# First RMS norm of a two-layer decoder: second tile of x transferred ahead of the weights, its statistics on another engine

## The chip, the cores and the metric

The kernel runs on one core of one Trainium2 chip. The metric is device time in microseconds (us) from the start to the end of one execution; lower is better. The core has TensorE (PE, matmuls and transposes), VectorE (DVE), ScalarE (ACT), GpSimd (POOL) and SyncE (SP, which issues most transfers); they run side by side, each through its own queue in order, and wait for each other through semaphores.

## The reference

Two decoder layers over x of 256 tokens by 1024 features, all in float32. Cut to what matters here:

```python
def rms_norm(x, g):
    y = x * lax.rsqrt(jnp.mean(x * x, axis=-1, keepdims=True) + NORM_EPS)
    return y * g

for l in range(DEPTH):                                  # 2
    h = rms_norm(x, attn_norm[l])                       # the norm of this change, for l = 0
    parts = jnp.split(h @ w_in[l], splits, axis=-1)     # 13 column groups
    # convolution module, compressed / selected / windowed attention, dilated attention
    x = x + jnp.concatenate([y_a, y_b, y_c], axis=-1) @ w_out[l]
    x = x + conv_ffn(rms_norm(x, ffn_norm[l]), w_up[l], ...)
```

## The kernel before

**Tiling.** x is held as two tiles of 128 tokens by 1024 features, called tile 0 and tile 1 (`x_sb[0]`, `x_sb[1]`). Each dense product is done as three matmuls on rounded halves: every operand is split into a high part (`hi`, written by ACT) and a remainder (`lo`, written by DVE as operand minus high part), and `dense3` (L441 to L443) adds hi*hi, hi*lo and lo*hi.

**Weights.** All weights lie in one stream of pieces, taken in order. A piece is transferred into one of four `raw` buffers (`raw_in`, L255), then `convert_piece` writes `whi` (ACT, L209) and `wlo` (DVE, L212) from it; the raw buffer is free for a later piece when `wlo` is written. Of layer 0, pieces 0 to 3 are the 280 columns of chunk `a0` (two of eight contraction blocks each, 280 KB), pieces 4 and 5 are `w1` (tile `w`, L282, 512 KB each, no split, buffers of their own), and pieces 6 to 9 are the 512 columns of chunk `a` (512 KB each). Piece 6 can so be issued when piece 0 has been split. `emit_piece` emits the next piece; `take` emits up to three pieces ahead.

**The first norm.** `norm_squares` sums the squares of a tile in two halves of 512 columns (tile 0: one half on ACT, one on DVE; tile 1: both on ACT). `norm_tile` then makes the mean, adds EPS, takes the inverse square root by a magic constant and three Newton steps (`rsqrt_into`; ten instructions on one column, named `na`, `nr`, `nwh`, `nwt`), scales each half by that and by the gain into `xn` (L222, DVE), transposes it in four 128x128 blocks on PE (L350, tile `tpx`) and splits the transposed half into `xT_hi` (ACT) and `xT_lo` (DVE). The gain of this norm lies in a PSUM bank: a matmul of a row of ones with the gain row (`gain`, L247) spreads it over the partitions. Matmuls of chunk `a0` for tile 0, then for tile 1, then those of chunk `a` follow (tile `A`).

**Order.** A planner orders the instructions of each engine when the kernel is built: it takes what it thinks ready, earlier lines first. `tc.issue_after(ins)` puts those instructions of its block that are on the engine of `ins` behind `ins` in that queue; it is order alone, not a wait. Pieces 0 and 1 are emitted between the squares of tile 1 and its `norm_tile`, piece 0 behind the scaling of tile 0 on DVE, piece 1 behind both splits of tile 0. SP's queue is in the order x tile 0, gain row, piece 0, x tile 1, pieces 1 to 3, then `w1`, the next gain, `w1`, piece 6, and after it the tables `feat`, `cst` and `ffeat` (339, 610 and 88 KB). POOL does little here: constants, small transfers, and `gain_tables` (tile `gsc`, twelve instructions for each layer, from the transferred `grow`, for which there is one buffer).

Of the kernel before, what the change touches and what calls it, by code (L numbers as in the profile page):

```python
# [12 lines left out]
F32 = mybir.dt.float32  # L13
F32R = mybir.dt.float32r
I32 = mybir.dt.int32
AF = mybir.ActivationFunctionType
ALU = mybir.AluOpType
AX = mybir.AxisListType

P = 128  # L20
D = 1024
# [6 lines left out]
EPS = 1e-6  # L28
BIG = 1e30
TAPS = 31  # L30
MAGIC = float(0x5F3759DF)
# [156 lines left out]
def tile_hybrid_trunk(ctx, tc, x_in, pos_in, stream, feats, gains, norms, const_in, out):  # L188
    nc = tc.nc
# [3 lines left out]
    sp = ctx.enter_context(tc.tile_pool(name="sp", bufs=2))  # L193
# [5 lines left out]
    def tp_bank(nm):  # L199
        return ps.tile([P, 512], F32, tag="tp", name=nm, bufs=2)  # L200
# [7 lines left out]
    def copy_act(o, i, **kw):  # L208
        return nc.scalar.activation(out=o, in_=i, func=AF.Copy, **kw)  # L209

    def tt(o, a, b, op):
        return nc.vector.tensor_tensor(out=o, in0=a, in1=b, op=op)  # L212

    def ts(o, a, s1, s2, op0, op1=None, eng=None):
        e = eng or nc.vector
        if op1 is None:
            e.tensor_scalar(out=o, in0=a, scalar1=s1, scalar2=None, op0=op0)
        else:
            e.tensor_scalar(out=o, in0=a, scalar1=s1, scalar2=s2, op0=op0, op1=op1)

    def stt(o, a, s, b, op0, op1):
        return nc.vector.scalar_tensor_tensor(out=o, in0=a, scalar=s, in1=b, op0=op0, op1=op1)  # L222
# [3 lines left out]
    def load_x(t):  # L226
        for h in range(2):
            nc.sync.dma_start(x_sb[t][:, h * 512:(h + 1) * 512], x_in[0, t * P:(t + 1) * P, h * 512:(h + 1) * 512])
# [21 lines left out]
    state = {"next": 0, "spare": {}, "gate": {}, "raw": {}}  # L250

    def raw_in(i):
        n = PIECES[i][3]
        raw = wp.tile([P, PIECE], F32, tag="raw", name=f"raw{i}", bufs=RAW_BUFS)
        nc.sync.dma_start(raw[:, :n], stream[OFFSETS[i]:OFFSETS[i] + P * n].rearrange("(p n) -> p n", p=P))  # L255
        return raw

    state["raw"][0] = raw_in(0)
    load_x(1)
    for i in (1, 2, 3):  # L260
        state["raw"][i] = raw_in(i)

    def slots(i):
# [37 lines left out]
        cursor["i"] += 1  # L301
        return emitted.pop(i)

    def rsqrt_into(y, a, shape, nm):
        h = sp.tile(shape, F32, tag="nwh", name=f"nwh{nm}", bufs=2)
        t = sp.tile(shape, F32, tag="nwt", name=f"nwt{nm}", bufs=2)
        ts(y.bitcast(I32), a.bitcast(I32), -0.5, MAGIC, ALU.mult, ALU.add)
        ts(h, a, -0.5, None, ALU.mult)
        one = shape[1] == 1
        for _ in range(3):  # L310
            if one:
                ts(t, y, y, h, ALU.mult, ALU.mult)
                ts(y, t, 1.5, y, ALU.add, ALU.mult)
            else:
                tt(t, y, y, ALU.mult)
                tt(t, t, h, ALU.mult)
                stt(y, t, 1.5, y, ALU.add, ALU.mult)
# [4 lines left out]
    def norm_squares(t, nm, out, split=False):  # L322
        x = x_sb[t]
        ss = sp.tile([P, 2], F32, tag="ss", name=f"ss{nm}", bufs=2)
        for h in range(2):
            sl = slice(h * 512, h * 512 + 512)
            if split and h:
                nc.vector.tensor_tensor_reduce(out=out[:, sl], in0=x[:, sl], in1=x[:, sl], op0=ALU.mult, op1=ALU.add, scale=1.0, scalar=0.0,
                                               accum_out=ss[:, h:h + 1])
            else:  # L330
                nc.scalar.activation(out=out[:, sl], in_=x[:, sl], func=AF.Square, accum_out=ss[:, h:h + 1])
        return ss

    def norm_tile(t, gi, nm, ss=None):
        x = x_sb[t]
        g = gain_tiles[gi]
        xn = sp.tile([P, D], F32, tag="xn", name=f"xn{nm}", bufs=1)
        if ss is None:
            ss = norm_squares(t, nm, xn)
        a = sp.tile([P, 1], F32, tag="na", name=f"na{nm}", bufs=2)  # L340
        ts(a, ss[:, 0:1], ss[:, 1:2], 1.0 / D, ALU.add, ALU.mult)
        ts(a, a, EPS, None, ALU.add)
        r = sp.tile([P, 1], F32, tag="nr", name=f"nr{nm}", bufs=2)
        rsqrt_into(r, a, [P, 1], nm)
        for h in range(2):
            sl = slice(h * 512, h * 512 + 512)
            scaled = stt(xn[:, sl], x[:, sl], r, g[:, sl], ALU.mult, ALU.mult)
            tp = tp_bank(f"tpx{nm}{h}")
            for k in range(4):
                nc.tensor.transpose(tp[:, k * P:(k + 1) * P], xn[:, h * 512 + k * P:h * 512 + (k + 1) * P], ident)  # L350
            tv = tp.rearrange("p (k c) -> p k c", k=4)
            hi = xT_hi[:, h * 4:h * 4 + 4, t * P:(t + 1) * P]
            lo = xT_lo[:, h * 4:h * 4 + 4, t * P:(t + 1) * P]
            ends = copy_act(hi, tv), tt(lo, tv, hi.bitcast(F32), ALU.subtract)
        return ends + (scaled,)
# [10 lines left out]
    nc.gpsimd.dma_start(freq, const_in[:, CONST_N:CONST_N + 32])  # L366
    junk = wp.tile([P, PIECE], F32, tag="whi", name="junk", bufs=W_BUFS)
    ss0 = norm_squares(0, "a00", junk, split=True)
    x_ready = norm_tile(0, 0, "a00", ss0)
    junk = wp.tile([P, PIECE], F32, tag="whi", name="junk1", bufs=W_BUFS)  # L370
    ss1 = norm_squares(1, "a01", junk)
    with tc.issue_after(x_ready[2].ins):
# [4 lines left out]
    for l in range(L):  # L377
        g = sp.tile([P, 4, 64], F32, tag="grow", name=f"grow{l}", bufs=1)
        nc.gpsimd.dma_start(g.rearrange("p a b -> p (a b)"), gains[l:l + 1, :].broadcast_to([P, 256]))
        grow.append(g)  # L380
    x_ready = norm_tile(1, 0, "a01", ss1)
    cos_t = cp.tile([P, 3, 32], F32, name="cos_t")
    sin_t = cp.tile([P, 3, 32], F32, name="sin_t")
    gs_t = []
# [108 lines left out]
    for l in range(L):  # L493
        f = sp.tile([P, NPF], F32, tag="feat", name=f"feat{l}", bufs=1)
# [318 lines left out]
        def conv_tail():  # L813
# [11 lines left out]
            ts(va, vp[:, 0:2], EPS, None, ALU.add)  # L825
            rs = mp.tile([P, 2], F32, name="rs")
            rsqrt_into(rs, va, [P, 2], f"ln{l}")
            dg = mp.tile([P, 2, P], F32, tag="cth", name="dg", bufs=1)
            bp = o_bank("lnb")
# [19 lines left out]
        def dil_qk(nm, jp):  # L849
            q = 2 if nm == "q" else 3  # L850
            dst = mp.tile([P, 3, S], F32, tag=f"d{nm}", name=f"d{nm}{jp}", bufs=1)
            dil_state[nm] = dst
            banks = tok_chunk(f"d{nm}{jp}", 384, False, f"D{nm}{jp}{l}")
            zrs = rope([b[:, 0:384] for b in banks], 6, q, (0, 1), f"d{nm}{jp}")
            for t in range(NT):
                tp = tp_bank(f"tpd{nm}{jp}{t}")
                for i in range(3):
                    nc.tensor.transpose(tp[:, i * P:(i + 1) * P], zrs[t][:, i * P:(i + 1) * P], ident)
                copy_act(dst[:, :, t * P:(t + 1) * P], tp[:, 0:384].rearrange("p (k c) -> p k c", k=3))
# [80 lines left out]
        for step in ORDER.split():  # L940
            nm, arg = step[:-1].split("(")
            arg = int(arg) if arg.isdigit() else arg.split(",")
            if nm == "dq":
                dil_qk("q", arg)
            elif nm == "dk":
                dil_qk("k", arg)
            else:
                dict(np=nsa_pair, t=conv_taps, nf=nsa_finish, dv=dil_v, da=dil_attn, ds=dil_scores, pv=dil_pv, ct=lambda _: conv_tail())[nm](arg)

# [25 lines left out]
        for t in range(NT):  # L975
            src = obs[t]
            for nh in range(2):
                sl = slice(nh * 512, nh * 512 + 512)
                tt(x_sb[t][:, sl], x_sb[t][:, sl], src[nh], ALU.add)
            ends = norm_tile(t, 2 * l + 1, f"f{l}{t}")  # L980
# [97 lines left out]
```

## Time and profile before

| | |
|---|---|
| median of 3 runs | 757.74 us (756.37 to 759.26) |
| profiled execution, time | 756.99 us |
| profiled execution, span from first to last instruction | 755.2 us |
| outside the span | 1.79 us |

The profile is of one execution. PE, DVE, ACT and POOL times are those of instructions; PEld is PE's weight load, beside its matmuls. A view by windows gives each engine's busy time in a stretch, with the count of instructions in brackets. The chain of waits follows the last instruction back, at each step to what released it. The ends of matmuls are modelled.

### The profile page before, as it was taken

How to read it: one execution, taken by the hardware profiler on the slowest of the kernel's cores; microseconds unless marked ns; L12 is line 12 of the kernel's file. 1: busy time of each engine (PE TensorE's matmuls, PEld its weight loads, DVE VectorE, ACT ScalarE, POOL GpSimd, SP SyncE). 2: the span in 40 equal slices, each digit the busy share in tenths (PEclk: the TensorE clock that was granted, in tenths of full speed). 3: DMA queues.
4: the chain of work that ended last, by engine and by line, in shares of the span. 5: the costliest groups of instructions: out<-in, count | busy, mean ns of one | idle time of the engine just before them, and what ended most of it. 6: DMA issues, size and time to landing. Idle time of an engine off the chain costs nothing.

```text
span 755.2 us, 13417 instructions
## 1 busy us (share of the span) xinstructions
PE 733.7 (97%) x4802; PEld 638.8 (85%) x4802; DVE 598.6 (79%) x1387; ACT 487.5 (65%) x1176; POOL 23.4 (3%) x57
## 2 busy tenths in 40 slices
PE   5999999999999999999999999999999999999997
PEld 4778776887899999988868977778789999999885
DVE  6889999986898888854487798998868988888441
ACT  3866998656586666643358589987538666666330
POOL 3300000000000000000040000000000000000000
PEclk9999999999999999999999999999999999999999
DMA  7754233245366656566447241235245665666631
GB/s 261 262 188 126 66 103 115 103 168 158 114 225 196 192 173 194 193 200 196 142 161 259 85 125 44 89 108 194 84 141 168 202 189 176 195 189 194 196 112 56
DMA packets 36005, 119.77 MB, mean 159 GB/s; under 512 B 4113, under 2 KB 4385, under 8 KB 35938
## 3 DMA queue, kind: packets, MB, share of 16 engines
q1 hardware_dynamic: 35714, 118.63, 49.2%
q8 instruction: 38, 0.62, 0.3%
q0 software_dynamic: 224, 0.28, 0.2%
q14 instruction: 29, 0.24, 0.1%
HBM read 117.85 MB, written 1.05 MB: 157 GB/s over the span
## 4 chain that ended last, share of the span: by engine, by line
PE 81%; DVE 8%; ACT 6%; DMA 3%; issue 2%; SPq 0%; DVEq 0%; ACTq 0%
PE up L442 10%; PE up L443 10%; PE up L441 10%; PE da L441 3%; PE da L442 3%; PE da L443 3%; PE db L441 3%; PE db L442 2%; PE db L443 2%; DVE wlo L212 2%; DMA raw<-in_stream 2%; ACT whi L209 2%; PE sc L742 1%; PE Dk L441 1%; PE Dk L443 1%
## 5 line engine op out<-in xcount | busy, mean ns | idle before, releaser
L212 DVE TENSOR_TENSOR wlo<-raw,whi 128x1024 fp32r<-128x1024 f32 (+3 forms) x232 | 259.8, 1125 | 88.8 <-ACT whi L209 88.1
L209 ACT ACTIVATE whi<-raw 128x1024 fp32r<-128x1024 f32 (+3 forms) x232 | 225.1, 980 | 108.7 <-PE db L443 54.5
L442 PE MATMUL up<-xT_lo,whi 128*128 128x256 f32 x640 | 178.9, 279 | 0.0
L443 PE MATMUL up<-xT_hi,wlo 128*128 128x256 f32 x640 | 178.9, 279 | 0.0
L441 PE MATMUL up<-xT_hi,whi 128*128 128x256 f32 x640 | 178.7, 279 | 0.0
L442 PEld LDWEIGHTS up<-xT_lo,whi 128*128 128x128 f32 x640 | 120.2, 188 | 0.0
L441 PEld LDWEIGHTS up<-xT_hi,whi 128*128 128x128 f32 x640 | 120.0, 188 | 0.0
L443 PEld LDWEIGHTS up<-xT_hi,wlo 128*128 128x128 f32 x640 | 119.9, 187 | 0.0
L222 DVE SCALAR_TENSOR_TENSOR u<-up,ffeat,u 128x255 f32<-128x255 f32 (+1 forms) x176 | 80.1, 479 | 2.6
L222 DVE SCALAR_TENSOR_TENSOR acc<-a_pad,dwh,acc 128x256 f32<-128x256 f32 x120 | 54.2, 480 | 0.3 <-ACT acc L706 0.2
L1031 ACT ACTIVATE sl<-u 128x256 f32<-128x256 f32 x44 | 18.1, 417 | 47.7 <-DVE u L222 47.7
L1024 ACT ACTIVATE u<-up,ffeat 128x256 f32<-128x256 f32 x88 | 44.2, 552 | 0.0
L441 PE MATMUL db<-whi,gT_hi 128*128 128x512 f32 x88 | 34.6, 393 | 0.0
L441 PE MATMUL da<-whi,gT_hi 128*128 128x512 f32 x88 | 34.6, 393 | 0.0
L442 PE MATMUL da<-wlo,gT_hi 128*128 128x512 f32 x88 | 34.4, 391 | 0.0
L442 PE MATMUL db<-wlo,gT_hi 128*128 128x512 f32 x88 | 34.4, 391 | 0.0
L443 PE MATMUL db<-whi,gT_lo 128*128 128x512 f32 x88 | 34.3, 390 | 0.0
L443 PE MATMUL da<-whi,gT_lo 128*128 128x512 f32 x88 | 34.3, 390 | 0.0
L441 PE MATMUL A<-whi,xT_hi 128*128 128x280 f32 (+1 forms) x64 | 23.2, 363 | 1.7 <-ACT xT_hi L209 1.7
L209 ACT ACTIVATE ms<-ms,dd 128x128 f32<-128x128 f32 (+1 forms) x64 | 24.3, 451 | 0.0
L443 PE MATMUL A<-whi,xT_lo 128*128 128x280 f32 (+1 forms) x64 | 22.9, 358 | 0.3 <-DVE xT_lo L212 0.3
L442 PE MATMUL A<-wlo,xT_hi 128*128 128x280 f32 (+1 forms) x64 | 23.0, 360 | 0.0
(342 smaller groups left out, 1572.7 us busy)
## 6 DMA issues: line engine op xcount, KB each, us to landing
raw<-in_stream SPq DMA_DIRECT2D x172, 512.0 KB, 4.1
raw<-in_stream SPq DMA_DIRECT2D x48, 384.0 KB, 3.1
raw<-in_stream SPq DMA_DIRECT2D x8, 280.0 KB, 4.3
w<-in_stream SPq DMA_DIRECT2D x4, 512.0 KB, 5.7
gain<-in_norms SPq DMA_DIRECT2D x3, 512.0 KB, 3.8
x<-in_x SPq DMA_DIRECT2D x4, 256.0 KB, 4.2
out<-x SPq DMA_DIRECT2D x4, 256.0 KB, 2.0
feat<-in_feats SPq DMA_DIRECT2D x2, 339.0 KB, 4.4
```

Source lines behind the costliest of these rows:

```text
L209: return nc.scalar.activation(out=o, in_=i, func=AF.Copy, **kw)
L212: return nc.vector.tensor_tensor(out=o, in0=a, in1=b, op=op)
L222: return nc.vector.scalar_tensor_tensor(out=o, in0=a, scalar=s, in1=b, op0=op0, op1=op1)
L441: nc.tensor.matmul(o, a_hi, b_hi, start=start, stop=False)
L442: nc.tensor.matmul(o, a_hi, b_lo, start=False, stop=False)
L443: nc.tensor.matmul(o, a_lo, b_hi, start=False, stop=stop)
L742: nc.tensor.matmul(sc[:, j * 512:j * 512 + n], QT[hp_, pair, P:2 * P], keys[hp_], start=True, stop=True)
L1024: nc.scalar.activation(out=u[:, h], in_=z, func=AF.Identity, scale=c[:, 2:3], bias=c[:, 3:4])
L1031: nc.scalar.activation(out=sl_, in_=u[:, 0], func=AF.Silu)
```

## The change

Tile 1 of x is transferred ahead of piece 0. The ten instructions on one column are taken out of `norm_tile` into `norm_rms`, which takes an engine; for tile 1 of the first norm that engine is POOL. The whole of that `norm_tile` is in a block that is queued behind `x_ready[1]`, the last `xT_lo` of tile 0: its DVE instructions, which are the two scalings and two `xT_lo`, come after it on DVE. Two single-operation instructions (adding EPS, and the product with -0.5) get a second operation, a product with 1.0, in every norm.

```diff
-    state["raw"][0] = raw_in(0)
     load_x(1)
-    for i in (1, 2, 3):
+    for i in range(4):
         state["raw"][i] = raw_in(i)
...
-    def rsqrt_into(y, a, shape, nm):
+    def rsqrt_into(y, a, shape, nm, eng=None):
...
-        ts(y.bitcast(I32), a.bitcast(I32), -0.5, MAGIC, ALU.mult, ALU.add)
-        ts(h, a, -0.5, None, ALU.mult)
+        ts(y.bitcast(I32), a.bitcast(I32), -0.5, MAGIC, ALU.mult, ALU.add, eng=eng)
+        ts(h, a, -0.5, 1.0, ALU.mult, ALU.mult, eng=eng)
...
-                ts(t, y, y, h, ALU.mult, ALU.mult)
-                ts(y, t, 1.5, y, ALU.add, ALU.mult)
+                ts(t, y, y, h, ALU.mult, ALU.mult, eng=eng)
+                ts(y, t, 1.5, y, ALU.add, ALU.mult, eng=eng)
...
+    def norm_rms(ss, nm, eng=None):
+        a = sp.tile([P, 1], F32, tag="na", name=f"na{nm}", bufs=2)
+        ts(a, ss[:, 0:1], ss[:, 1:2], 1.0 / D, ALU.add, ALU.mult, eng=eng)
+        ts(a, a, EPS, 1.0, ALU.add, ALU.mult, eng=eng)
+        r = sp.tile([P, 1], F32, tag="nr", name=f"nr{nm}", bufs=2)
+        rsqrt_into(r, a, [P, 1], nm, eng)
+        return r
...
-    x_ready = norm_tile(0, 0, "a00", ss0)
+    x_ready = norm_tile(0, 0, "a00", norm_rms(ss0, "a00"))
...
-    x_ready = norm_tile(1, 0, "a01", ss1)
+    with tc.issue_after(x_ready[1].ins):
+        x_ready = norm_tile(1, 0, "a01", norm_rms(ss1, "a01", nc.gpsimd))
```

## Rows read from the trace of the kernel before

**Rows 1.** The page: the span, and each engine's busy time in it.

```profile
span 755.2 us, 13417 instructions
PE 733.7 (97%) x4802; PEld 638.8 (85%) x4802; DVE 598.6 (79%) x1387; ACT 487.5 (65%) x1176; POOL 23.4 (3%) x57
```

**Rows 2.** Windows: busy PE, PEld, DVE, ACT, POOL; granted clock, DMA share, GB/s.

```profile
0.00:20.00 20.00, 12.01 (x44) 8.11 (x44) 12.31 (x40) 8.21 (x20) 7.11 (x25) 1.00 0.80 269
...
40.00:60.00 20.00, 20.00 (x112) 16.83 (x113) 17.97 (x51) 13.43 (x57) 0.00 (x0) 1.00 0.50 153
```

**Rows 3.** Chain of waits, first 25 us: start, us, what.

```profile
2.43 5.35 DMA x<-in_x
...
10.57 0.75 DVE xna L222
...
14.08 5.41 DMA raw<-in_stream
...
19.60 1.15 ACT whi L209 x2
...
21.28 0.39 PE A L441
...
23.38 0.13 PE A L442
```

**Rows 4.** Timeline of DVE, first 20 us: start, duration, what, idle before.

```profile
7.11 0.21 DVE L219 TENSOR_SCALAR nra<-nwta,nra 128x1 f32<-128x1 f32 x1
9.69 0.21 DVE L219 TENSOR_SCALAR naa<-ssa 128x1 f32<-128x1 f32 x1 [2.37 <-ACT junk L331]
...
13.82 0.20 DVE L212 TENSOR_TENSOR wlo<-raw,whi 128x48 fp32r<-128x48 f32 x1
14.06 0.69 DVE L212 TENSOR_TENSOR xT_lo<-tpxa,xT_hi 128x512 fp32r<-128x512 f32 x1
...
17.70 1.41 DVE L222 SCALAR_TENSOR_TENSOR xna<-x,nra,gain 128x512 f32<-128x512 f32 x2
```

**Rows 5.** Timeline of all engines: the gain matmul, the next gain's transfer, PE's last `a0` matmul.

```profile
4.01 3.75 PE L247 MATMUL gain<-grow_n,one_row 1*128 1x512 f32 x4 [4.01 <-DMA grow_n<-in_norms]
...
7.79 0.33 SPq L236 DMA_DIRECT2D gain<-in_norms  x1
...
18.17 0.29 PE L443 MATMUL A<-whi,xT_lo 128*128 128x280 f32 x1
```

**Rows 6.** Transfers issued at 2.04 (piece 0) and 2.43 (x): KB, us to landing.

```profile
raw<-in_stream SPq DMA_DIRECT2D x1, 280.0 KB, 5.2
...
x<-in_x SPq DMA_DIRECT2D x1, 256.0 KB, 5.4
```

**Rows 7.** Windows of 5 us, columns as in rows 2.

```profile
10.00:15.00 5.00, 3.54 (x14) 3.11 (x15) 4.32 (x11) 2.17 (x5) 3.32 (x13) 1.00 0.78 302
15.00:20.00 5.00, 4.72 (x28) 3.83 (x26) 4.14 (x14) 2.05 (x7) 0.00 (x0) 1.00 0.88 282
20.00:25.00 5.00, 3.72 (x25) 3.53 (x26) 4.67 (x14) 2.96 (x7) 0.81 (x2) 1.00 1.03 413
```

**Rows 8.** Windows cut at PE's stages: `a0` of tile 0, the gap, the rest.

```profile
13.20:18.50 5.30, 5.26 (x25) 4.54 (x24) 5.21 (x16) 2.56 (x7) 0.42 (x1) 1.00 0.67 187
18.50:21.28 2.78, 1.26 (x8) 0.84 (x8) 1.70 (x5) 2.34 (x6) 0.81 (x2) 1.00 1.03 415
21.28:42.65 21.37, 20.32 (x119) 16.91 (x120) 18.91 (x42) 17.44 (x40) 6.62 (x8) 1.00 0.73 248
```

**Rows 9.** POOL's timeline, and the instructions of tile `gsc` (ns min/median/max).

```profile
10.00 2.72 POOL L219 TENSOR_SCALAR gsc<-grow 128x64 f32<-128x64 f32 x12 [5.27 <-DMA grow<-in_gains]
...
L219 POOL TENSOR_SCALAR gsc<-grow x24: 208/208/872, 10.0 to 383.6; 128x32 f32<-128x32 f32 x16, 128x64 f32<-128x64 f32 x8
```

**Rows 10.** ACT's timeline: the squares of tile 1 around the first `whi`.

```profile
7.80 0.63 ACT L331 ACTIVATE junk<-x 128x512 f32<-128x512 f32 x1 [3.51 <-DMA x<-in_x]
...
9.47 0.19 ACT L331 ACTIVATION_READ_ACCUMULATOR junk<-x 128x1 f32 x1
```

More of the change, by code (lines that the diff above doesn't have):

```diff
@@ L332, in norm_squares, with norm_tile @@
         return ss
-    def norm_tile(t, gi, nm, ss=None):
+    def norm_rms(ss, nm, eng=None):
[5 more added lines that the diff above has]
+        return r
+    def norm_tile(t, gi, nm, r=None):
         x = x_sb[t]
@@ L337, in norm_tile @@
         xn = sp.tile([P, D], F32, tag="xn", name=f"xn{nm}", bufs=1)
[L338 to L344, printed above, removed]
+        if r is None:
+            r = norm_rms(norm_squares(t, nm, xn), nm)
         for h in range(2):
```

## The prediction

> **What bounds the kernel now.** I read the page first, for how full PE is. It is busy for 733.7 of 755.2 us [rows 1], so a change at the start can win at most what PE loses there. Next the windows of 20 us, to find where it loses: PE is busy for 12.01 us of the first 20 and for all of 40 to 60 [rows 2]. From about 43 us on it is full, so whatever stands earlier there should stand earlier at the end, and the question is by how much the work before 43 us moves.
>
> Then the chain of waits over the first 25 us [rows 3]. It runs: the transfer of x tile 1 (2.43 to 7.78), the squares of tile 1 on ACT, the first statistics of tile 1 on DVE, and only at 10.57 the scaling of tile **0**. From there tile 0 goes through its transposes and split to the end of piece 0's split, which lets piece 6 be issued at 14.08. Its transfer takes 5.41, ACT splits it from 19.60, then splits tile 1's transpose, and PE has its first `a0` matmul of tile 1 at 21.28.
>
> The timeline of DVE says why tile 0 waits for tile 1. The factor of tile 0 is ready at 7.32 (7.11 and 0.21), but five instructions of tile 1's statistics stand next in DVE's queue, and the first of them waits 2.37 us for tile 1's squares [rows 4]. The gain bank is not what holds the scaling: its matmuls end at 7.76, and the next gain's transfer, which needs that buffer, was issued at 7.79 [rows 5].
>
> **The change part by part.**
>
> *Statistics of tile 1 off DVE.* With them gone the first scaling can start when the factor is ready, at 7.40 with the usual 0.08 to the next instruction, in place of 10.57: a gain of 3.17. If its first half has to wait for the modelled end of the whole gain matmul, 7.76, it starts at 7.85 and the gain is 2.72. I take 3.17, since the first half needs only the first half of the bank; 2.72 stays as the bound.
>
> *What follows tile 0.* The chain from 10.57 to 14.08 is work, so piece 6 is issued at 10.91. It landed 5.41 after issue with three tables issued right behind it. Now it meets `w1` and the next gain. Windows of 5 us show 302 and 282 GB/s from 10 to 20 against 413 from 20 to 25 [rows 7]; the 1510 KB moved from 10 to 15 would at that best rate be done by 13.7. Two bounds: the 512 KB of piece 6 alone after that land at 14.9; piece 6 with its three tables, 1549 KB, lands at 17.4. The present 5.41 gives 16.32, between them, and I take that. ACT then splits it, and tile 1's `a0` matmuls start at 21.28 less 3.17, 18.11.
>
> *Later pieces.* What the transfers leave unused from 10 to 20 is 5 us at 111 GB/s and 5 us at 131 GB/s, 1210 KB, which is 2.9 us at 413 GB/s [rows 7]. The stream up to about 25 us can so move up by 2.9, not by 3.17. I take 0.2 off for it. From 21.28 to 42.65 PE is busy for 20.32 of 21.37 us [rows 8], so the shift is kept.
>
> *x ahead of piece 0.* Piece 0 was issued at 2.04 and landed after 5.2, tile 1's first half was issued at 2.43 and landed after 5.4 [rows 6], that is at 7.24 and 7.83. With 280 KB fewer in front, at the same 413 GB/s, x lands 0.7 earlier at best and no later than now. The squares end 9.66 now (9.47 and 0.19 [rows 10]), with one `whi` between them; in a row and 0.7 earlier they end at about 8.6. Piece 0, behind 512 KB more, lands at about 8.5 at the latest; its `whi` is then written from 8.6 to 9.3, and the first matmul of tile 0 would come at 10.0 (its stage begins at 13.2 [rows 8], less 3.17). That covers it; without the cover, each us beyond 0.7 would come off the gain.
>
> *Ten instructions on POOL.* The trace has none of this shape there. The nearest are the twelve of `gsc`, 2.72 us in a row at 10.00, 0.227 each; over both layers the median is 0.208 and the longest 0.872 [rows 9]. Ten cost 2.1 to 8.7 us; I take 2.3, as the shape is smaller and the first twelve ran so. Tile 1's factor would be ready at 10.9 (17.3 at the upper bound). It is needed when DVE comes to tile 1's scaling, behind the last `xT_lo` of tile 0, which ends at 14.75 now [rows 4] and at 11.58 then: 0.7 to spare, so nothing.
>
> The longest of those instructions bears on that: the same operation took four times its median at one place and not at others [rows 9]. A rule for such a thing is in the Trainium skill, page "SBUF — State Buffer", section "Who interferes with whom": a VectorE instruction with two SBUF inputs and a GpSimd one that reads SBUF exclude each other, and the later one waits for the whole of the other. By it, every `wlo` on DVE could hold a POOL instruction back, and ten at the longest duration make the 17.3 above, with which the sum shrinks to 0.4 (rival two); by the median row it does not change.
>
> *The order block and the second operations.* Order behind `xT_lo` costs nothing of itself, since the scaling waits for POOL anyway. The product with 1.0 is two more operations in eight norms, in instructions that exist; a product and a sum in one instruction is already the form of the first statistic, 0.21 for one column [rows 4]. Between nothing and 0.06 for each, 1 us at most if every one were on the path; I take nothing, since PE is full around most of them.
>
> **Sum.** 3.17 less 0.2 is 3.0 us earlier. The profiled execution has a span of 755.2, so 752.2 after, and 754.0 with the 1.79 outside it; it lies 0.75 below the median of the runs. Against the median, 757.74 less 3.0 is **754.7 us**, 0.4% faster. About 0.5%, 3.8 us, is what a measurement of this kernel can tell from no change: the bounds are 753.9 and 761.5.
>
> **The rivals.**
>
> *One: more comes free.* PE's gap before tile 1 is 2.78 long with 1.26 of transposes in it [rows 8]. It is there because ACT takes piece 6 ahead of tile 1's transpose. If tile 1 is scaled at 11.6 and split ahead of piece 6, the idle 1.52 goes as well: 4.7 in all, 753.0. The matmuls of tile 0 are also far apart: 24 of them fill most of 5.3 us [rows 8], while later ones come every 0.13 [rows 3], 3.1 for 24, at a granted clock of 1.00 (2.4 GHz) in either stretch; if PE gets them in its faster pace, up to 2.2 more, 750.8. For it: DVE loses both the stall and the ten instructions. Against it: the splits of pieces 1 to 3 must still pass DVE. Chance 0.26.
>
> *Two: POOL is late.* Either `gsc` stands first, and the ten start at 12.72 and end at 15.0, or they run at 0.872. At 17.3 tile 1 is scaled 0.4 earlier than now (17.70 [rows 4]): 757.3. For it: POOL's queue is in order, and its first `gsc` waits for a transfer until 10.00 [rows 9], later than 8.6. Chance 0.16 for a gain under 2.
>
> *Three, the other side: DVE waits for POOL with other work behind.* The scaling of tile 1 (1.41) may stand in DVE's queue ahead of the splits of pieces 1 to 3, about 2.7 us (three times 0.69, as for an `xT_lo` of that shape, and 0.20 [rows 4]). With the factor ready at T, the last split ends at T + 4.1. Now it ends ahead of 17.70, where tile 1's scaling starts, and PE's last matmul of tile 0 follows at 18.17 [rows 4, 5]; so tile 0 gets later from T = 13.6. As tile 1 then follows without the gap of 2.78, the end gets later from T = 16.4. At 17.3 it is 0.9 later, 758.6; past 20.2, more than 3.8 later. Chance 0.12, half of it past that.
>
> *Four: the change does not do what it says.* Something else holds the scaling of tile 0 at 10.57, or a new stall before 43 us takes the gain: 757.7. The row of the gain bank speaks against the first. Chance 0.06.
>
> **How the numbers follow.** The forecast, a gain of 2 to 3.8, has 0.40. Of all cases, rival one (and 0.02 of the forecast's edge) is faster by over 0.5%: 0.28. Slower by over 0.5% is half of rival three and 0.01 of the rest: 0.07. The remaining 0.65 is within 0.5%. For the range I leave out a third of rival one below 752.2 (0.09) and most of rival three above 758.3 (0.10), and take in the rest, the 2.72 and the late POOL among it.
>
> **What would show it.** In the timeline of DVE after: the first scaling at about 7.4 with no wait for ACT before it; piece 6 issued near 10.9; the transfers without the dip before 16; tile 1's first `a0` matmul near 18.1; POOL's ten instructions from 8.6 to 11. The prediction is wrong if tile 1's scaling waits for POOL, if piece 6 still lands past 18, or if PE has a new gap between 25 and 43 us.

## The result and the profile after

The changed kernel takes 754.09 us in the median of 7 runs (752.9 to 755.91), the kernel before, run beside it, 757.33 (756.37 to 759.81). The ratio is 0.9948, 95% interval 0.9932 to 0.9964: 3.2 us faster, between 2.7 and 5.1. The forecast was 754.7 with a range from 752.2 to 758.3. The span of the profiled execution went from 755.2 [rows 1] to 751.2, 4.0 us less. Runs of one kernel differ by some 2 us with their mean granted clock (in the changed kernel 752.9 at 1.000 and 755.91 at 0.994), so a median moves with how many runs lie at the lower end (in e4 below eight of twelve under 0.998, in e5 four).

The page and the first window show where it went. Columns of the window: busy PE, PEld, DVE, ACT, POOL; granted clock, DMA share, GB/s.

```profile
span 751.2 us, 13420 instructions
PE 733.9 (98%) x4802; PEld 639.5 (85%) x4802; DVE 597.3 (80%) x1377; ACT 487.0 (65%) x1176; POOL 25.5 (3%) x67
```

```profile
0.00:20.00 20.00, 14.61 (x64) 11.05 (x65) 14.15 (x41) 10.12 (x24) 11.12 (x37) 1.00 0.90 314
```

PE's sum is that of before (733.7 [rows 1]). In the first 20 us it is busy for 14.61 in place of 12.01 [rows 2]: the same work, begun earlier.

The timeline of DVE after (start, duration, what, idle before):

```profile
7.35 0.21 DVE L219 TENSOR_SCALAR nra<-nwta,nra 128x1 f32<-128x1 f32 x1
8.00 1.41 DVE L222 SCALAR_TENSOR_TENSOR xna<-x,nra,gain 128x512 f32<-128x512 f32 x2 [0.43 <-PE gain L247]
9.32 0.69 DVE L212 TENSOR_TENSOR wlo<-raw,whi 128x512 fp32r<-128x512 f32 x1
...
11.50 0.69 DVE L212 TENSOR_TENSOR xT_lo<-tpxa,xT_hi 128x512 fp32r<-128x512 f32 x1
12.10 0.84 DVE L212 TENSOR_TENSOR wlo<-raw,whi 128x512 fp32r<-128x512 f32 x2
12.87 1.40 DVE L222 SCALAR_TENSOR_TENSOR xna<-x,nra,gain 128x512 f32<-128x512 f32 x2
```

The wait of 2.37 us for tile 1's squares and the five instructions behind it [rows 4] are gone. The first scaling starts at 8.00 in place of 10.57, 2.57 earlier, and waits 0.43 for the gain matmul. Tile 1's scaling comes at 12.87 in place of 17.70, with no wait before it. POOL's timeline says why that was possible:

```profile
8.26 0.26 POOL L219 TENSOR_SCALAR naa<-ssa 128x1 f32<-128x1 f32 x1 [3.53 <-ACT junk L330]
...
9.42 0.80 POOL L219 TENSOR_SCALAR nwta<-nra,nwha 128x1 f32<-128x1 f32 x1
...
10.69 0.33 POOL L219 TENSOR_SCALAR nwta<-nra,nwha 128x1 f32<-128x1 f32 x1
11.13 0.27 POOL L219 TENSOR_SCALAR nra<-nwta,nra 128x1 f32<-128x1 f32 x1
11.49 0.34 POOL L219 TENSOR_SCALAR nwta<-nra,nwha 128x1 f32<-128x1 f32 x1
11.94 0.27 POOL L219 TENSOR_SCALAR nra<-nwta,nra 128x1 f32<-128x1 f32 x1
12.16 2.02 POOL L219 TENSOR_SCALAR gsc<-grow 128x64 f32<-128x64 f32 x8
```

The ten stand ahead of `gsc` and take 3.95 us, from 8.26 to 12.21: longer than the 2.3 taken in the prediction, and done 0.66 before DVE needs the factor.

ACT's timeline and PE's, from tile 1's squares to its first `a0` matmul:

```profile
6.35 0.63 ACT L330 ACTIVATE junk<-x 128x512 f32<-128x512 f32 x1 [1.85 <-DMA x<-in_x]
...
7.97 0.19 ACT L330 ACTIVATION_READ_ACCUMULATOR junk<-x 128x1 f32 x1
8.06 0.75 ACT L209 ACTIVATE whi<-raw 128x512 fp32r<-128x512 f32 x2
...
15.22 1.09 ACT L209 ACTIVATE xT_hi<-tpxa 128x512 fp32r<-128x512 f32 x2 [1.80 <-PE tpxa L352]
16.19 1.15 ACT L209 ACTIVATE whi<-raw 128x512 fp32r<-128x512 f32 x2
```

```profile
10.66 0.60 PE L444 MATMUL A<-whi,xT_hi 128*128 128x280 f32 x1
...
14.41 1.21 PE L352 MATMUL tpxa<-ident,xna 128*128 128x128 f32 x8
15.87 0.40 PE L444 MATMUL A<-whi,xT_hi 128*128 128x280 f32 x1 [0.25 <-ACT xT_hi L209]
```

In the chain of before, ACT split piece 6 and only then tile 1's transpose [rows 3]. Now `xT_hi` of tile 1 (15.22) stands ahead of piece 6's `whi` (16.19). Tile 1's transposes stand in the middle of tile 0's `a0` matmuls, and PE starts tile 1 at 15.87 in place of 21.28. Its idle time just before that is 0.25. Of the 5.41 between the two starts about 1.4 is order alone: 11 of tile 0's 24 matmuls now come behind tile 1's first, 0.13 each. The windows cut at PE's stages, as in rows 8, say the same:

```profile
10.66:14.40 3.74, 3.74 (x14) 3.26 (x14) 3.69 (x9) 2.55 (x7) 3.40 (x14) 1.00 1.02 402
14.40:15.87 1.47, 1.22 (x10) 0.97 (x8) 0.72 (x2) 0.65 (x2) 1.17 (x4) 1.00 1.03 373
15.87:38.80 22.93, 21.75 (x130) 18.38 (x131) 20.86 (x50) 18.90 (x42) 6.50 (x11) 1.00 0.80 263
```

The stage between the tiles was 2.78 us with 1.26 of work [rows 8]; it is 1.47 with 1.22. The chain of waits over the same stretch (start, us, what):

```profile
8.26 0.27 POOL naa L219
...
8.89 1.94 PE tpxa L352 x8
...
14.61 0.59 PE tpxa L352 x4
...
15.22 0.61 ACT xT_hi L209
...
15.87 0.40 PE A L444
```

The transfer of piece 6 and the two `whi` that followed it [rows 3] are no part of it any more. (The step from POOL to the transposes joins two things that did not wait for each other; the transposes waited for the scaling on DVE.) The windows of 5 us show that the transfers moved up:

```profile
10.00:15.00 5.00, 5.00 (x21) 4.28 (x20) 4.32 (x10) 3.15 (x8) 4.49 (x17) 1.00 1.02 401
15.00:20.00 5.00, 4.75 (x37) 4.47 (x36) 4.25 (x15) 2.87 (x7) 1.47 (x5) 1.00 1.04 357
20.00:25.00 5.00, 5.00 (x29) 4.12 (x28) 4.97 (x12) 4.16 (x11) 0.00 (x0) 1.00 0.76 292
```

From 10 to 20 they ran at 401 and 357 GB/s in place of 302 and 282 [rows 7]. Piece 6 was issued at 11.52 in place of 14.08 and landed after 4.2 us, not 5.41.

Chunk `b`, the next behind `a`, begins at 38.64 on PE; before it began at 42.49. Of these 3.85 us, 2.57 are tile 0's start and 1.16 PE's wait just ahead of tile 1 (1.41 in the timeline of before, 0.25 after); a wait of 0.23 ahead of the `hid` matmuls went too, and the wait ahead of the first `cmp` matmul grew from 0.81 to 1.18. That makes 3.59; 0.26 I can't place.

### The profile page after: what moved, and what is told of

Its sections match the earlier page's. It is cut to its first block, busy times and chain, and to the rows that moved or that the text cites. A ratio compares the mean times of both kernels' runs of the same rounds, so it can differ in the third digit from the quotient of the medians.

```text
span 751.2 us, 13420 instructions
## 1 busy us (share of the span) xinstructions
PE 733.9 (98%) x4802; PEld 639.5 (85%) x4802; DVE 597.3 (80%) x1377; ACT 487.0 (65%) x1176; POOL 25.5 (3%) x67
## 4 chain that ended last, share of the span: by engine, by line
PE 84%; DVE 6%; ACT 5%; DMA 2%; issue 2%; SPq 0%; DVEq 0%; POOL 0%; ACTq 0%
PE up L445 10%; PE up L444 10%; PE up L446 10%; PE da L444 3%; PE da L446 3%; PE da L445 3%; PE db L444 3%; PE db L446 3%; PE db L445 2%; DVE wlo L212 2%; DMA raw<-in_stream 2%; PE sc L745 1%; ACT whi L209 1%; PE Dk L444 1%; PE Dk L446 1%
## 5 line engine op out<-in xcount | busy, mean ns | idle before, releaser
L444 PE MATMUL Dq<-whi,xT_hi 128*128 128x384 f32 x64 | 23.0, 359 | 0.0
```

The lines of the kernel that those rows point to most:

```text
L444: nc.tensor.matmul(o, a_hi, b_hi, start=start, stop=False)
```

## The experiments

All times in us. The first five columns are of each kernel's profiled execution; the difference is that of the median to the median of the kernel before on the same chip, and the interval that of their ratio. An interval is some 2.4 us wide, so two kernels less than about 1.7 us apart are not told apart by their intervals. The column of tile 1's first `a0` matmul has two kinds of kernel in it: in before, e4, e5 and e9 all 24 of tile 0's matmuls come ahead of it, in the others 13.

| kernel | tile 0 scaled | tile 1 scaled | tile 1's first `a0` | first `b` | span | difference | ratio, interval |
|---|---|---|---|---|---|---|---|
| before | 10.57 | 17.70 | 21.28 | 42.49 | 755.2 | | |
| changed | 8.00 | 12.87 | 15.87 | 38.64 | 751.2 | -3.24 | 0.9948, 0.9932 to 0.9964 |
| e1 changed, again | 8.07 | 13.06 | 15.98 | 38.75 | 751.2 | -4.18 | 0.9950, 0.9934 to 0.9967 |
| e2 transfer order alone | 10.52 | 15.33 | 17.82 | 40.67 | 754.0 | -1.54 | 0.9981, 0.9966 to 0.9996 |
| e3 piece 0 first | 7.88 | 15.23 | 17.44 | 40.23 | 752.7 | -3.58 | 0.9957, 0.9942 to 0.9973 |
| e4 statistics on DVE, behind | 7.64 | 16.57 | 19.96 | 42.70 | 756.6 | +2.05 | 1.0026, 1.0014 to 1.0038 |
| e5 e4, one table load fewer | 7.84 | 17.23 | 19.59 | 40.92 | 754.5 | -2.05 | 0.9982, 0.9968 to 0.9996 |
| e6 POOL longer | 7.92 | 15.72 | 17.93 | 42.13 | 754.3 | -1.15 | 0.9986, 0.9972 to 1.0 |
| e7 gain row by ACT | 7.83 | 13.88 | 16.09 | 42.83 | 755.6 | -4.10 | 0.9955, 0.994 to 0.9971 |
| e8 PE busy before | 8.07 | 13.06 | 15.56 | 38.05 | 751.6 | -4.55 | 0.9946, 0.9932 to 0.996 |
| e9 changed, without POOL | 7.85 | 15.98 | 18.30 | 40.83 | 753.8 | -1.15 | 0.9983, 0.9968 to 0.9998 |
| e10 tanh table early | 7.86 | 13.31 | 15.52 | 39.11 | 753.3 | -3.79 | 0.9950, 0.9935 to 0.9965 |
| e11 e7 and e8 | 7.87 | 13.31 | 15.53 | 39.73 | 752.9 | -2.40 | 0.9971, 0.9955 to 0.9986 |

All diffs are against the changed kernel. **e1** is that kernel itself, run beside e2 to e4.

> The changed kernel as it is, beside the three that undo parts of it. Every theory expects what was measured before: a ratio near 0.995, the first scaling near 8.0 us, tile 1's scaling near 12.9, the first matmul of chunk b near 38.6 us (42.5 in the kernel before).

It came out as in the result, within the interval.

**e2: the transfer order alone.** Tile 1's statistics are on DVE and nothing is queued behind anything.

```diff
-    with tc.issue_after(x_ready[1].ins):
-        x_ready = norm_tile(1, 0, "a01", norm_rms(ss1, "a01", nc.gpsimd))
+    x_ready = norm_tile(1, 0, "a01", norm_rms(ss1, "a01"))
```

> Only x tile 1 ahead of piece 0; the ten statistics of tile 1 stay on DVE, and all ten stand ahead of tile 0's scaling in its queue. Theory one (the gain has two parts: 2.6 us from tile 0's scaling no longer waiting behind tile 1's statistics, and some 1.3 us from PE's gap before tile 1, which closes when tile 1 is split ahead of piece 6): the first scaling is at about 10.6 as before, piece 6 is issued near 14.1, but tile 1 follows without the gap, so the first matmul of chunk b comes near 41.2 and the kernel is 1.3 us faster than before. Rival (the order of the transfers makes the gain): 3.9 us faster. Rival (all comes from tile 0's scaling): no change.

DVE, and PE between the tiles:

```profile
8.27 0.21 DVE L219 TENSOR_SCALAR naa<-ssa 128x1 f32<-128x1 f32 x1 [0.90 <-ACT junk L330]
...
10.39 0.21 DVE L219 TENSOR_SCALAR nra<-nwta,nra 128x1 f32<-128x1 f32 x1
10.52 1.40 DVE L222 SCALAR_TENSOR_TENSOR xna<-x,nra,gain 128x512 f32<-128x512 f32 x2
```

```profile
17.82 0.39 PE L443 MATMUL A<-whi,xT_hi 128*128 128x280 f32 x1 [0.25 <-ACT xT_hi L209]
```

All ten instructions now stand ahead of tile 0's scaling, so that it gains nothing (10.52). Yet tile 1 is scaled 2.37 earlier, ACT takes it ahead of piece 6, and PE's wait goes from 1.41 to 0.25: 1.8 earlier at chunk `b`. Closing that gap pays without any release of tile 0. (Some 0.3 of the 1.8 is the pace of tile 0's matmuls: the 13th starts 0.34 earlier, at 16.40 in place of 16.74, with the first only 0.06 earlier.)

**e3: piece 0 transferred first,** the rest of the change kept.

```diff
+    state["raw"][0] = raw_in(0)
     load_x(1)
-    for i in range(4):
+    for i in (1, 2, 3):
```

> Statistics of tile 1 on POOL, but piece 0 is transferred ahead of x tile 1, as before. Theory one: the first scaling stays at 8.0, the squares of tile 1 end near 9.7, POOL's ten take 3.9 us to 13.6, tile 1's scaling moves from 12.9 to 13.6 or 13.7 with DVE idle for 0.8, and at most that 0.8 us is lost: 3.1 to 3.9 us faster than before. Rival (the order of the transfers makes the gain, or most of it): under 1.5 us faster.

DVE's timeline:

```profile
7.88 1.41 DVE L222 SCALAR_TENSOR_TENSOR xna<-x,nra,gain 128x512 f32<-128x512 f32 x2 [0.55 <-PE gain L247]
10.53 0.69 DVE L212 TENSOR_TENSOR wlo<-raw,whi 128x512 fp32r<-128x512 f32 x1 [1.24 <-ACT whi L209]
...
15.23 1.41 DVE L222 SCALAR_TENSOR_TENSOR xna<-x,nra,gain 128x512 f32<-128x512 f32 x2 [1.35 <-POOL nra L219]
```

With x behind piece 0, tile 1's squares are late (9.25 on ACT, not 6.35). Piece 0's `whi` waits behind the first of them on ACT, so tile 0's first `a0` matmul comes at 11.77 and not at 10.66, and then DVE waits 1.35 for POOL. In the profile that is 1.5 us of span; the two differences to before lie 0.6 apart, which the intervals don't tell from nothing.

**e4: no POOL, piece 0 first.** As e3, with tile 1's statistics on DVE, behind the last split of tile 0.

```diff
-        x_ready = norm_tile(1, 0, "a01", norm_rms(ss1, "a01", nc.gpsimd))
+        x_ready = norm_tile(1, 0, "a01", norm_rms(ss1, "a01"))
```

> Piece 0 ahead of x tile 1 as before, the ten statistics on DVE, but all of tile 1's DVE work is queued behind the last split of tile 0. Theory one: the first scaling is at 8.0 and piece 6 issued at 11.5, but tile 1's scaling comes behind the splits of pieces 1 to 3, near 15.1, and ACT takes piece 6 ahead of tile 1's transpose, so the gap on PE stays: 2.6 us faster than before, the first matmul of chunk b near 39.9. Rival (POOL is needed for the gain at all): no faster than before. Rival (only taking DVE's stall away matters): 3.9 us faster, as the changed kernel.

My theory one fell: tile 0 is scaled 2.93 earlier than in the kernel before, and the kernel is slower. ACT's timeline shows a first cause:

```profile
34.84 0.28 ACT L529 ACTIVATE sin_t<-trig 128x96 f32<-128x96 f32 x1
...
35.45 1.28 ACT L660 ACT_TABLE_LOAD   x1
36.74 0.23 ACT L660 ACTIVATE ht<-hz 128x32 f32<-128x32 f32 x1
...
37.93 1.28 ACT L529 ACT_TABLE_LOAD   x1
39.23 0.28 ACT L529 ACTIVATE cos_t<-trig 128x96 f32<-128x96 f32 x1
39.53 0.31 ACT L209 ACTIVATE hv<-hk 64x128 f32<-64x128 f32 x1
```

The planner now puts the tanh of `ht` between the sine and the cosine of the rotation tables. ACT loads its function tables three times in place of two, 1.28 each, the third ahead of `hv`, for which PE waits 1.45.

**e5: e4 with the tanh queued behind the cosine.** Its own lines, beside those of e4:

```diff
-                    nc.scalar.activation(out=t_.rearrange("p a b -> p (a b)"), in_=r_, func=AF.Sin)
+                    state["cos"] = nc.scalar.activation(out=t_.rearrange("p a b -> p (a b)"), in_=r_, func=AF.Sin)
...
-            nc.scalar.activation(out=ht, in_=hz, func=AF.Tanh, scale=0.5)
+            with tc.issue_after(state["cos"].ins) if split else ExitStack():
+                nc.scalar.activation(out=ht, in_=hz, func=AF.Tanh, scale=0.5)
```

> As e4 (statistics of tile 1 on DVE, behind the last split of tile 0), but the tanh of ACT that makes ht is queued behind the cosine, so that ACT changes its table once between the sine and ht, not three times. In e4 the first hid matmul was 1.6 us earlier than in the kernel before and the first of chunk b 0.2 later, with PE waiting 1.45 for hv behind a table load of 1.28. Theory two (e4 lost its gain to the planner's order on ACT, through that load): chunk b starts near 41.2 and the kernel is 1.3 us faster than e4 at least, so no slower than before by more than 0.7 and up to 1.3 faster. Rival (the loss is in moving DVE's work itself, the slower pace of the matmuls or the gap): as e4, 1 to 2 us slower than before.

One load fewer, chunk `b` 1.78 earlier, the span 2.1 shorter, and the difference to before goes from +2.05 to -2.05. Of the 1.78, 1.45 is PE's wait for `hv`, gone; 0.32 is there at the `hid` matmuls already, where tile 0's matmuls had come 0.23 apart to the end in e4 and 0.13 apart from 15.9 in e5. So the order on ACT made most of e4's loss. That the medians moved by twice what `b` did is explained in part only, by the granted clock: at 0.998 and above the two differences to before lie 3.1 apart, not 4.1.

**e6: POOL made longer,** by three more Newton steps (16 instructions in place of 10).

```diff
-        for _ in range(3):
+        for _ in range(3 if eng is None else 6):
```

> The changed kernel with six Newton steps on POOL in place of three: 16 instructions, not ten; the order of all queues stays. The six more take about 2.4 us (0.8 for a pair in the changed kernel), so tile 1's factor comes at about 14.6 and DVE waits 1.7 for it with the splits of pieces 2 and 3 behind. Theory (rival three of the prediction, that a late POOL costs what stands behind it on DVE, one for one): tile 1's scaling at 14.6, chunk b near 40.3, 1.7 us slower than the changed kernel, 2.2 faster than before. Rival (PE has enough queued that POOL has slack): no more than 0.4 slower than the changed kernel.

POOL and DVE:

```profile
11.99 0.90 POOL L219 TENSOR_SCALAR nwta<-nra,nwha 128x1 f32<-128x1 f32 x1
```

```profile
12.03 0.80 DVE L212 TENSOR_TENSOR wlo<-raw,whi 128x512 fp32r<-128x512 f32 x2
15.72 1.41 DVE L222 SCALAR_TENSOR_TENSOR xna<-x,nra,gain 128x512 f32<-128x512 f32 x2 [2.88 <-POOL nra L219]
```

DVE waits 2.88 us, and behind that wait stand the splits of pieces 2 and 3, much as in rival three. PE waits 2.08 in turn, then does its `a0` matmuls at 0.23 each up to 21.69 (granted clock 0.84 and 0.82 in the windows from 15 to 25). Against e1 the price is 3.0 us for a tile 1 scaled 2.7 later, about one for one. The 1.7 expected was for a factor at 14.6; it came at 15.68, since the squares ended 0.4 later than in the changed kernel's profile and two of the sixteen instructions were held by DVE, not one. In this execution the lower clock is part of the price too. Faster than before it still is: chunk `b` begins at 42.13, there at 42.49.

**e7 and e8: the start of PE.** e7 transfers the gain row through ACT's queue; e8 puts six small matmuls of ones around the gain matmul (five ahead of it).

```diff
-    nc.sync.dma_start(grow0, norms[0:1, :])
+    nc.scalar.dma_start(grow0, norms[0:1, :])
```

```diff
+    wz = cp.tile([P, P], F32, name="wz")
+    nc.vector.memset(wz, 1.0)
+    wb = mm_bank("warm")
+    for _ in range(5):
+        nc.tensor.matmul(wb[:, 0:P], wz, wz, start=True, stop=True)
...
+    nc.tensor.matmul(wb[:, 0:P], wz, wz, start=True, stop=True)
```

> The changed kernel with the transfer of the gain row issued from ACT's queue at the start, in place of third on SP's. Theory (the modelled end of the gain matmul is real, and the whole of it holds the first scaling, 0.43 us): the gain matmul starts near 3.3, the first scaling comes as soon as the factor of tile 0 is ready, 7.6 in place of 8.0, and chunk b and the end are 0.4 us earlier than in the changed kernel. Rival (the first scaling waits for something else): it stays at 8.0.

> The changed kernel with six 128-column matmuls of ones, into a bank that nothing reads, ahead of the gain matmul on PE. Theory (the matmuls of tile 0 come every 0.23 us until about 16.2 and every 0.13 after, because PE did little before them, and that costs): with PE busy from 1.5 us on they come every 0.13 earlier, and the end is up to 1.4 us earlier than in the changed kernel, less what the splits on DVE hold back. Rival (the pace does not follow what PE did before 9 us, or DVE's splits are the bound there): no change within 0.4.

In e7 the wait of 0.43 for the gain bank is gone, but the factor itself comes at 7.72, so the scaling starts 0.17 earlier only. Tile 1's second half of x is then squared at 8.52, not 7.43, and DVE waits 1.15 for POOL. Neither kernel differs measurably from the changed one. In e8 the fast pace of PE starts at 14.1, in the changed kernel at 14.8 (the last section says how that is read; the expectation took it at 16.2), and chunk `b` 0.6 earlier, and the span has none of it. That the small matmuls made the earlier pace is not shown: e9 and e10 have it at 13.9 and 14.0 without them.

**e9: the change without POOL.** Only the ten instructions go back to DVE, in the same block; the tanh is fenced as in e5.

```diff
-        x_ready = norm_tile(1, 0, "a01", norm_rms(ss1, "a01", nc.gpsimd))
+        x_ready = norm_tile(1, 0, "a01", norm_rms(ss1, "a01"))
```

> The changed kernel with tile 1's ten instructions back on DVE, queued behind the last split of tile 0 like the scaling (x still ahead of piece 0; the tanh queued behind the cosine, so that the third table load of e4 does not come back). First scaling near 8.0 as in the changed kernel. Theory one (POOL buys the closing of PE's gap): on DVE the ten stand among the splits of pieces 1 to 3, tile 1's scaling comes near 16, ACT takes piece 6 ahead of tile 1's transpose and PE's gap stays; tile 1's first a0 matmul near 19.4, time 755.5 to 756.3. Theory two (the release of tile 0 is all of the gain): tile 1's lateness is absorbed before 43 us, time 753.5 to 754.2.

PE's waits:

```profile
16.88 1.29 PE L352 MATMUL tpxa<-ident,xna 128*128 128x128 f32 x8 [1.20 <-DVE xna L222]
...
38.79 0.27 PE L667 MATMUL cmp<-feat,hk 64*32 64x64 f32 x2 [1.98 <-issue]
```

Theory one holds in what it says of POOL: without it the kernel loses 2.1 us of the gain against the result and 3.0 against e1, and the spans lie 2.6 apart. The gap stays, but for another reason than expected. ACT does take piece 6 first (16.53, tile 1's `xT_hi` at 17.65), yet PE waits 1.20 for the scaling on DVE ahead of the transposes and 0.13 behind them: it is tile 1's late scaling that costs. This kernel is close to what the sum of the prediction assumed: tile 0 released at 7.85 and tile 1's first `a0` matmul at 18.30 (forecast 7.40 and 18.11). That lead of 2.98 at tile 1 is 1.66 at chunk `b`: PE waits 1.98 for `hk`, against 0.81 before. ACT writes `ht` there at 37.59, hardly earlier than before (37.71), behind a `whi` that waited 1.12 for its transfer, the sine (34.43), the cosine and two table loads. Part of what e9 loses is this order on ACT, the tanh's fence included; no run took that out alone.

**e10: tanh's table early.** A tanh on one column behind the cosine, which is kept in `state` as in e5.

```diff
+            if split:
+                pre = mp.tile([P, 1], F32, name="pre")
+                with tc.issue_after(state["cos"].ins):
+                    nc.scalar.activation(out=pre, in_=cos_t[:, 0, 0:1], func=AF.Tanh, scale=0.5)
```

> The changed kernel with one tanh on one column queued behind the cosine, so that the table load (1.28 us) stands ahead of the hid matmuls and not between hz and ht. Theory one: PE's wait of 1.18 us ahead of the first cmp matmul (34.28) is the price of that load; it shrinks to under 0.3 and the time is 752.4 to 753.0. Theory two: ACT is full there (4.9 of 5 us) and in the new order a whi of 1.04 us stands between hz and ht in place of the load, so hk comes as late as before and the time stays at 753.2 to 754.2.

```profile
35.79 0.27 PE L670 MATMUL cmp<-feat,hk 64*32 64x64 f32 x2 [1.42 <-issue]
```

Theory two, and one thing more: the load left its place between `hz` and `ht`, a `whi` (32.98) came in, and on DVE a `wlo` (34.07 to 35.36) now stands ahead of the two instructions that make `hk`. PE waits 1.42, no less than the 1.18 of the changed kernel.

**e11: e7 and e8 together,** a try at a version better than the changed one.

> The changed kernel with the edits of e7 and e8 together: the gain row by ACT's queue and six small matmuls of ones around the gain matmul. Theory one (PE is bound by later steps before 43 us): the lead at the start of tile 0 and in the pace of the a0 matmuls is used up before chunk b's end, time 753.3 to 754.3, as for each of the two alone. Theory two (leads at the start reach the end): first scaling 0.2 to 0.4 earlier, pace of 0.13 from about 14, chunk b near 37.9, time 752.4 to 753.0.

```profile
27.96 3.76 PE L657 MATMUL hid<-flat,w 128*128 128x64 f32 x32 [1.12 <-issue]
```

Neither theory: it lies nearer to before than both parts. PE waits 1.12 ahead of `hid`, since on ACT the last three `flat` copies stand behind a `whi` and the load for the sine and start at 27.14. e7 has the same order and a wait of 1.48 there, and a better median; why they differ is open. No version beat the changed kernel measurably.

## Why the prediction was right, and where only the number was

**The wait that goes.** Right in kind: in the kernel before, DVE held a finished factor behind tile 1's statistics. The size was the wrong end: I took 3.17 and kept 2.72 as a bound, for the case that the first half of the scaling waits for the whole gain matmul. It does (0.43 idle), and x of tile 0 landed 0.2 later, so the term is 2.57.

**"The shift is kept."** This step was too simple. A release of tile 0 alone (e9) was 2.98 ahead at tile 1 and 1.66 at chunk `b`; e4, also ahead at tile 1 by 1.32, was slower than before. The sum used PE's busy share from 21.28 to 42.65, 20.32 of 21.37; but that share holds for the order of before. When the work arrives in another order, the planner lays ACT's queue out otherwise, and PE gets new waits at `hid` and `cmp`.

**PE's gap.** The sum left it in place and kept its closing for rival one. It closed, by rival one's mechanism: tile 1's `xT_hi` ahead of piece 6 on ACT. That is worth 1.16 in the profile; e2, without the release, shows 1.8 at chunk `b` and 1.5 in the median. So what was named the forecast, tile 0's release with the gap kept, is nearest to e9, with 1.15 in the median and 1.4 in the span, and what happened is the release and most of rival one. The forecast's time came out, at 0.6 us, because the release was worth less and the gap, which the sum kept, closed: two errors of opposite sign, and in so far luck. Rival one's other part, the faster pace for tile 0's matmuls, did not come: the 13 that run ahead of tile 1's transposes are mostly 0.23 apart.

**POOL.** The ten took 3.95, inside the bounds of 2.1 to 8.7 but far from the 2.3 chosen; their start at 8.26 (forecast 8.6) and a scaling of tile 1 that came 1.3 later than forecast (12.87, not 11.6) covered it. That DVE holds POOL back bears out in the trace: the longest, 0.80, runs from 9.42 to 10.22 beside the `wlo` of 9.32 to 10.01, its like are 0.33 and 0.34. In e6 the 0.68 at 9.30 stands beside the `wlo` of 9.25 to 9.93, the 0.90 at 11.99 beside those of 12.03 to 12.83. Two beside `xT_lo` (10.64 to 11.33, which reads PSUM and SBUF) stay at 0.33 and 0.27 (10.69 and 11.13). This is the rule of the Trainium skill, page "SBUF — State Buffer", section "Who interferes with whom", that was weighed in the prediction: the trace agrees, at about 0.5 us for one meeting. Rival two's case, `gsc` first, did not come: `gsc` waited behind.

The 0.66 to spare is that of one execution, in which one of the ten was held. In e1, the same kernel, two were, and in e10, whose edit lies far behind, two as well. The last of the ten and tile 1's scaling in e1, then the scaling in e10:

```profile
12.30 0.73 POOL L219 TENSOR_SCALAR nra<-nwta,nra 128x1 f32<-128x1 f32 x1
```

```profile
13.06 1.41 DVE L222 SCALAR_TENSOR_TENSOR xna<-x,nra,gain 128x512 f32<-128x512 f32 x2
```

```profile
13.31 1.41 DVE L222 SCALAR_TENSOR_TENSOR xna<-x,nra,gain 128x512 f32<-128x512 f32 x2 [0.54 <-POOL nra L219]
```

POOL ends at 13.03 in e1 and DVE starts at 13.06; in e10 DVE waits 0.54, which the prediction named as a sign of being wrong. So its "0.7 to spare, so nothing" held in the profiled execution, barely in e1, and not in e10.

**Rival three** is what e6 made: there POOL's factor is ready at 15.68 (15.41 and 0.27), and DVE waits with splits behind. The text let the end get later than before from 16.4 only, so at 15.68 the kernel should be 0.7 faster than before; it is 1.15 (interval 0 to 2.1). So the bound held. What it did not say is how soon a late POOL costs against the changed kernel: past 0.66 us of slack in one execution and 0.03 in another, about one for one.

**The transfers** kept pace: 401 GB/s from 10 to 15 is near the 413 taken as the best, and the loss of 0.2 for later pieces can't be seen. x landed by 7.41, the squares ended 8.16 (forecast 8.6), piece 0's `whi` followed at once: x ahead of piece 0 cost nothing, and without it (e3) POOL would have been late.

**The second operations,** taken at nothing, cost nothing: tile 0's ten on DVE take 2.32 us with them (5.24 to 7.56) and took 2.32 without (5.00 to 7.32).

## What to carry to other kernels

When a queue is freed, ask which of the things behind it comes next at the bottleneck: here freeing tile 0 alone (e9) gave 1.2 us by the medians and 1.4 by the spans, and 2.1 to 3.0 more came with tile 1 being scaled early, before ACT turned to the next piece. A chain of one-column instructions can go to an idle slow engine if its end lies ahead of the consumer's turn; past that point it costs about one for one (e6), and the slack should be read from more than one execution. In a planned kernel, look at the whole order of every engine after an edit: one table load in a new place cost PE 1.45 us (e4), over a third of what the edit won at chunk `b`.

## What the hardware showed

One-column instructions cost more on POOL by their pitch: the ten take 3.95 us, 3.5 without the one that was held, against 2.32 for tile 0's ten on DVE (5.24 to 7.56).

The matmuls of 280 columns start every 0.23 us at first, 1.2 columns a ns, and every 0.13 later, while the rows of both stretches read a granted clock of 1.00 (2.4 GHz). One column a cycle at the lower level, 1.2 GHz, would give the slow pace, but the rows don't show that level there. The change of pace came at about 16.8 in the kernel before and 14.8 in the changed one, in the middle of tile 1's transposes: eight of them take 1.94 us from 8.89 on and 1.21 from 14.41 on. It came at 14.1 in e8, 13.9 in e9 and 12.9 in e11; e8 and e11 had the small matmuls from 1.19 on, e9 had none. So these runs don't show what sets the place. In some profiled executions the granted clock itself fell later on, as in e10 at 37.8, behind a wait of PE of 1.42 that ended at 35.79 (window as above); in e9 it did not fall behind a wait of 1.98:

```profile
35.00:40.00 5.00, 4.21 (x17) 3.17 (x18) 4.79 (x17) 3.19 (x12) 0.00 (x0) 0.78 0.86 274
```

In the windows of 1 us from 38 to 41 it reads 0.50, and chunk `b`'s first matmuls there are 0.43 apart for 512 columns, later 0.23. The profile of e7 has such a stretch from 30 to 40 (0.63 and 0.69), so its span of 755.6 and its chunk `b` at 42.83 stand above what its median says.
